# Two embedding products moved one pass earlier, six blocks multiplied earlier, two rows scaled on ScalarE

## The chip, the core and the metric

The kernel runs on one core of a Trainium2 chip. The metric is the device time of one execution in microseconds (us). Besides the execution times there is one profiled execution of the kernel before.

## What is computed

One layer with sliding-window attention, then a gated embedding, then a norm. The change touches only what follows the attention's output product, where `x` has 512 rows and 2048 columns:

```python
x = x + y                                        # y: the attention's output product
emb = p[i] @ ple_proj[i]                         # 512x256 @ 256x2048
g = jax.nn.sigmoid(rmsnorm(x, ple_norm[i]) @ ple_gate[i])   # 512x2048 @ 2048x2048
x = x + emb * g
return rmsnorm(x, final_g)
```

Every float32 product is made of three products of rounded numbers: each operand is split into a high part and the rest (`hi`, `lo`), and hi x hi, hi x lo and lo x hi are summed in PSUM.

## The kernel before

**Blocks.** `x1[j][:, t, :]` holds rows 128t to 128t+127 and columns 512j to 512j+511 of `x`, for t and j from 0 to 3: 16 blocks. "Row t" below means these 128 rows.

**The gate product** uses Strassen's seven products over a two by two division. They are passes, in the order P2, P7, P1, P6, P5, P3, P4. Passes P2 to P3 have two units each (`jj` = 0, 1, the two column halves); `unit()` takes four weight pieces, and with each piece 12 matmuls of 128x512 into two PSUM banks (`tb` = 0, 1). P4 is written out by hand in `block()`: half of a unit each, called for (0, 0), (1, 0), (0, 1), and (1, 1) in two parts of 256 columns.

**Weight pieces.** The class `Pieces` (object `B`) runs a list of 128x1024 pieces in order. A piece is loaded on SP's queue (`braw`, three buffers), or has been summed in a `grown` buffer by adding DMAs on POOL's queue. Then ScalarE casts it to its high part (`bhi`, L575) and VectorE subtracts (`blo`, L576). `get(i)` has pieces up to i+2 split and up to i+3 loaded. `bhi` and `blo` have three buffers each, so a cast waits until TensorE is through with the piece three places before. P4's eight pieces are split ahead of use by `split_last(k)` (L583, L584) into tiles `spare`, `last`, `low`; the dictionary `early` says after which piece of which unit.

**The embedding.** `embed(t, w, tag)` makes one block of `emb`: six matmuls into a bank of the pair `tag`. Passes P1, P5, P3 have two such blocks behind each unit, from one piece of `ple_proj`: P1 gates rows 0 and 1 in columns j = 0, 1; P5 rows 2 and 3 in j = 2, 3; P3 rows 0 and 1 in j = 2, 3; P4 rows 2 and 3 in j = 0, 1. P5 and P3 use the same two pieces of `ple_proj`, and load and split them twice. PSUM has four pairs of banks, s, p, t and o. P1, P6, P5 and P3 add up their gate products in s and p; the embeddings take t for the first unit and o for the second.

**Gating a block** is a generator in three steps, `gated()`: sigmoid on ScalarE (L896); multiply by `emb` and add to `x` on VectorE (L898, L899); square with a sum on ScalarE (L902). `gate()` first adds the products that belong to the block.

**Order.** From P7 on the order of all five engines is the order of the program text. What belongs to a finished unit is put on the list `later`, and `some_later()` runs a share of it after each of the four pieces of the next unit. So the instruction queues of ScalarE and VectorE mix the casts and subtractions of coming pieces with the gating of the unit before. `Forms.steps` adds the left operands of the next pass (`hT`, `fhg`, `flg`; L668, L680, L681).

**The last norm.** `rsqrt_mean()` makes 1/sqrt of the mean square: the mean on VectorE, `rt` by a square root on ScalarE (L158), then a correction step on VectorE. It is called for rows 0 and 1 together once P3 is gated, and for row 2. Row 3 has its own lines at the end (L1088 to L1094). The square root and the sigmoid need different tables, so ScalarE loads a table before each of them (`ACT_TABLE_LOAD`). A block is finished by `row()`, one VectorE instruction that multiplies by the root and by the weights `fg` (L920), or by `by_gain()` (L912, by the weights, on VectorE) and a later multiplication by the root. `store()` sends it out on SP's queue.

Of the kernel before, what the change touches and what calls it, by code (L numbers as in the profile page):

```python
# [11 lines left out]
F32 = mybir.dt.float32  # L12
# [8 lines left out]
P = 128  # L21
KC = D // P
NB = S // P
# [30 lines left out]
def trunk_kernel(ctx: ExitStack, tc: tile.TileContext, a: dict):  # L54
    nc = tc.nc

    def pool(name, bufs=1, **kw):
        return ctx.enter_context(tc.tile_pool(name=name, bufs=bufs, **kw))
# [3 lines left out]
    const = pool("const")  # L62
# [18 lines left out]
    def bank(name, tag):  # L81
        return others.get(tag, psum).tile([P, 512], F32, tag=tag, name=name)
# [34 lines left out]
    def mm3(ps, sh, sl, mh, ml, first, last, more=False):  # L117


        nc.tensor.matmul(ps, sh, mh, start=first, stop=False, skip_group_check=more)  # L120
        nc.tensor.matmul(ps, sh, ml, start=False, stop=False, skip_group_check=more)  # L121
        nc.tensor.matmul(ps, sl, mh, start=False, stop=last, skip_group_check=more)  # L122
# [23 lines left out]
    def run(gen):  # L146
        for _ in gen:
            pass

    def rsqrt_mean(out, ssq, n, nm):  # L150

        w = out.shape[-1]
        ms = const.tile([P, w], F32, name=f"ms_{nm}")
        rt = const.tile([P, w], F32, name=f"rt_{nm}")
        y = const.tile([P, w], F32, name=f"y_{nm}")
        t = const.tile([P, w], F32, name=f"t_{nm}")
        nc.vector.tensor_scalar(ms, ssq, 1.0 / n, EPS, op0=ALU.mult, op1=ALU.add)
        nc.scalar.activation(rt, ms, AF.Sqrt)  # L158
        yield
        nc.vector.reciprocal(y, rt)  # L160
        nc.vector.tensor_mul(t, y, y)
        nc.vector.tensor_mul(t, t, ms)
        nc.vector.tensor_scalar(t, t, -0.5, 1.5, op0=ALU.mult, op1=ALU.add)
        nc.vector.tensor_mul(out, y, t)
# [20 lines left out]
    for k in range(KC):  # L185
# [9 lines left out]
        room = acts if k < KC // 2 else more  # L195
# [14 lines left out]
        f, e = k == 0, k == KC - 1  # L210
# [8 lines left out]
        for t in range(2):  # L219
            c = slice(t * P, (t + 1) * P)  # L220
            mm3(kt_ps[t], wh[:, c], wl[:, c], h, l, f, e)
        for t in range(NB):
            c = slice(t * P, (t + 1) * P)
# [8 lines left out]
        if 3 <= k < 3 + NB:  # L232
            t = k - 3
# [283 lines left out]
    def blk(t):  # L517
        return slice(t * P, (t + 1) * P)
# [9 lines left out]
    def block(nm, r, c, jj, m):  # L528
        return a[nm][2 * (c - 1) + jj, 4 * (r - 1) + m]

    SUMS = [("w_out", 7), ("w_out", 5), ("w_out", 6), ("ple_gate", 7), ("ple_gate", 5)]
    for nm, p in SUMS:
        for jj in range(2):
            for m in range(4):
                t = summed[nm, p, jj, m] = tc.dram_tile([P, WE], F32, name=f"{nm}_{p}_{jj}_{m}")
# [12 lines left out]
    class Pieces:  # L548
# [38 lines left out]
        done = 0  # L587
# [26 lines left out]
    def add_stage(nm, order):  # L614
        at = {}

        def add_embeds(p, jj):
            if nm == "ple_gate" and p in (1, 5, 3, 4):
                j = jj + 2 * (p in (5, 3))
                B.add("proj", a["ple_proj"].rearrange("(k p) d -> p k d", p=P)[:, :, j * 512 : (j + 1) * 512])  # L620

        for p in order:
            for jj in range(2):
                if nm == "ple_gate" and (p, jj) == (4, 0):
                    for v in range(2):
                        at["e", v] = len(B.specs)
                        add_embeds(p, v)
                at[p, jj] = len(B.specs)
                for m in range(4):
                    if (nm, p) in SUMS:  # L630
                        src = summed[nm, p, jj, m]
                    else:
                        src = block(nm, *{1: (1, 1), 2: (2, 1), 3: (2, 2), 6: (1, 1), 4: (2, 1)}[p], jj, m)
                    growing = (6, 4) if (nm, 6) in SUMS else (7, 6, 4)
                    kind = "seed" if p == growing[0] else "grow" if p in growing else "one"
                    B.add(kind, src, (nm, jj, m) if p in growing else None)
                if p != 4:
                    add_embeds(p, jj)
        return at
# [108 lines left out]
    late = pool("late", reuse_waits="tile")  # L748
    rooms.append(late)
    x1s = late.tile([P, 4, NB, 512], F32, name="x1s")  # L750
    x1 = [x1s[:, j] for j in range(4)]
    fg = late.tile([P, D], F32, name="fg")
    pTh = late.tile([P, 2, S], F32R, name="pTh")
    pTl = late.tile([P, 2, S], F32R, name="pTl")
    ssq2 = const.tile([P, NB, 4], F32, name="ssq2")
    ssq3 = const.tile([P, NB, 5], F32, name="ssq3")

# [12 lines left out]
    later = []  # L770
# [26 lines left out]
    def partial(nm):  # L797
        return late.tile([P, 2, 2, 512], F32, tag="partial", name=nm, bufs=2)
# [45 lines left out]
    for n, p in enumerate(ORDER_OUT):  # L844
        nxt = out_forms.steps(ORDER_OUT[n + 1]) if n < 6 else iter(())
        for jj in range(2):
# [3 lines left out]
            def todo():  # L850
                part = x_at.get((p, jj, next(calls)))
                if part is not None:
                    load_x(part)
                next(nxt, None)
                if p == 4:
                    for tag in "to":
                        if turns:
                            turn(*turns.pop(0), tag)
                    if jj:
                        next(ple_first, None)  # L860
# [21 lines left out]
    nc.vector.tensor_sub(pTl, pT, pTh.bitcast(F32))  # L882
    done = {t: 0 for t in range(NB)}

    def embed(t, w, tag, c=slice(0, 512)):
        e_ps = bank(f"e{t}_{done[t]}", tag)
        for k in range(2):
            mm3(e_ps[:, c], pTh[:, k, blk(t)], pTl[:, k, blk(t)], w[0][k][:, c], w[1][k][:, c], k == 0, k == 1)
        return e_ps
# [18 lines left out]
    def gain(j):  # L908
        return fg[:, j * 512 : (j + 1) * 512]

    def by_gain(t, j):
        nc.vector.tensor_mul(x1[j][:, t, :], x1[j][:, t, :], gain(j))  # L912

    def store(t, j):
        nc.sync.dma_start(a["out"][t * P : (t + 1) * P, j * 512 : (j + 1) * 512], x1[j][:, t, :])

    def row(t, j, yn):

        xt = x1[j][:, t, :]
        nc.vector.scalar_tensor_tensor(out=xt, in0=xt, scalar=yn, in1=gain(j), op0=ALU.mult, op1=ALU.mult)  # L920

    s2, s7 = partial("s2"), partial("s7")
    turns = [(kp, 1) for kp in range(4)]

    def gate(p, jj, ps, e):
# [17 lines left out]
                zs.append((tb, 2 + jj, ps[tb], late.tile([P, 512], F32, tag="junk", name=f"z{jj}_{tb}", bufs=3)))  # L943
        return [gated(*z, e[z[0]]) for z in zs]

    def gate_later(*v):
        zs = gate(*v)
        later[:0] = [partial_of(next, z, None) for _ in range(3) for z in zs]
# [2 lines left out]

    spare = late.tile([P, 2 * WE], F32R, name="spare")
    rooms4 = {}
    early = {(5, 0, 3): 0, (5, 1, 2): 1, (5, 1, 3): 2, (3, 0, 1): 3, (3, 0, 3): 4, (3, 1, 0): 5, (3, 1, 2): 6}

    def split_last(k):
        if k == 0:
# [4 lines left out]
        lo = late.tile([P, WE], F32R, tag="grown", name=f"low{k}", bufs=8)  # L962
        B.split_last(k, rooms4[(k - 1) // 2][:, (k - 1) % 2 * WE : ((k - 1) % 2 + 1) * WE], lo)

    for n, p in enumerate(ORDER_PLE[:-1]):
        if n == 1:

            ctx.enter_context(
                tc.manual_schedule(
                    engines={getattr(mybir.EngineType, v) for v in ("PE", "SP", "DVE", "Activation", "Pool")}  # L970
                )
            )
        nxt = ple_forms.steps(ORDER_PLE[n + 1])
        for jj in range(2):
            calls = iter(range(4))

            def todo():
                k = early.get((p, jj, next(calls)))
                if turns:
                    turn(*turns.pop(0), "s")  # L980
                    if not turns:
                        nc.vector.tensor_reduce(ss2, ssq2, axis=AX.X, op=ALU.add)
                        run(rsqrt_mean(rstd2, ss2, D, "r2"))
                    return
                next(nxt, None)
                if p == 2:
                    next(nxt, None)
                if k is not None:
                    split_last(k)

            ps = unit(p, jj, at_ple, ple_forms, todo)
            e = {}
            if p in (1, 5, 3):
                w = B.get(at_ple[p, jj] + 4)
                for t in (0, 1) if p in (1, 3) else (2, 3):
                    e[t] = embed(t, w, "to"[jj])
            if (p, jj) != (3, 1):
                later.insert(0, partial_of(gate_later, p, jj, ps, e))
        run(nxt)
    while later:  # L1000
        later.pop(0)()
# [2 lines left out]
    w = [B.get(at_ple["e", jj]) for jj in range(2)]  # L1004
    f = ple_forms.made[4]
# [26 lines left out]
    yn2 = const.tile([P, 3], F32, name="yn2")  # L1032
# [4 lines left out]
    g = block(0, 0, "s", "o")()  # L1037
    run(root)
    next(g)
    for j in range(4):  # L1040
        row(0, j, yn2[:, 0:1])
        store(0, j)
    next(g)
    run(g)
    for j in range(4):
        row(1, j, yn2[:, 1:2])
        store(1, j)
    g = block(1, 0, "s", "t")()
    next(g)
    for j in (2, 3):  # L1050
        by_gain(2, j)
    next(g)
    run(g)
    for j in (2, 3):
        by_gain(3, j)
    nc.vector.tensor_reduce(ssum[:, 2:], ssq3[:, 2, :4], axis=AX.X, op=ALU.add)
    root = rsqrt_mean(yn2[:, 2:], ssum[:, 2:], D, "r4")
    next(root)
# [9 lines left out]
    next(g)  # L1068
    run(g)

    base, ms, rt, im, ys, nw, yn = (const.tile([P, 1], F32, name=f"{v}_3") for v in ("base", "ms", "rt", "im", "ys", "nw", "yn"))
    g = block(1, 1, "p", "t", slice(0, 256))()
    next(g)
    by_gain(3, 0)
# [86 lines left out]
```

## Time and profile before

| | us |
|---|---|
| median of 3 runs (lowest to highest) | 804.19 (804.07 to 805.76) |
| the profiled execution's own time | 804.26 |
| its span, first to last instruction | 802.4 |
| busy: TensorE, VectorE, ScalarE, GpSimd | 791.1, 592.1, 500.5, 110.1 |

PE is TensorE, DVE VectorE, ACT ScalarE, SPq the queue of SP. A timeline row has the start, the duration (both us), engine, line, operation, the tiles written and read, the shape, and the number of equal instructions; a bracket gives the idle time before it and what ended it. Matmuls are pipelined: a row of 0.39 us starts 0.23 us after the one before. Times are counted from the span's start.

### The profile page before, as it was taken

How to read it: one execution, taken by the hardware profiler on the slowest of the kernel's cores; microseconds unless marked ns; L12 is line 12 of the kernel's file. 1: busy time of each engine (PE TensorE's matmuls, PEld its weight loads, DVE VectorE, ACT ScalarE, POOL GpSimd, SP SyncE). 2: the span in 40 equal slices, each digit the busy share in tenths (PEclk: the TensorE clock that was granted, in tenths of full speed). 3: DMA queues.
4: the chain of work that ended last, by engine and by line, in shares of the span. 5: the costliest groups of instructions: out<-in, count | busy, mean ns of one | idle time of the engine just before them, and what ended most of it. 6: DMA issues, size and time to landing. Idle time of an engine off the chain costs nothing. (4 is left out here: it accounts for less than half of the span.)

```text
span 802.4 us, 10946 instructions
## 1 busy us (share of the span) xinstructions
PE 791.1 (99%) x3763; PEld 660.0 (82%) x3763; DVE 592.1 (74%) x970; ACT 500.5 (62%) x1041; POOL 110.1 (14%) x218
## 2 busy tenths in 40 slices
PE   9999999999999999999999999999999999999995
PEld 7888888888888888888888888888888888888785
DVE  4536886887777776777778897766646756989896
ACT  5624667676667666676666654655668656656855
POOL 0002213122122212112122200030000020200000
PEclk9999999999999999999999999999999999999998
DMA  8863678778687977868685369898513996785532
GB/s 318 327 172 101 183 241 215 228 202 233 172 220 215 218 215 199 221 177 246 159 219 132 105 233 348 333 275 248 195 46 92 372 216 197 156 229 182 182 107 105
DMA packets 45239, 165.15 MB, mean 206 GB/s; under 512 B 5936, under 2 KB 8112, under 8 KB 41344
## 3 DMA queue, kind: packets, MB, share of 16 engines
q1 hardware_dynamic: 38352, 130.59, 47.9%
q0 software_dynamic: 6832, 33.88, 22.4%
q8 instruction: 29, 0.48, 0.2%
q14 instruction: 26, 0.21, 0.1%
HBM read 158.63 MB, written 46.19 MB: 255 GB/s over the span
## 5 line engine op out<-in xcount | busy, mean ns | idle before, releaser
L576 DVE TENSOR_TENSOR blo<-braw,bhi 128x1024 fp32r<-128x1024 f32 x80 | 97.5, 1222 | 39.7 <-ACT bhi L575 39.4
L575 ACT CAST bhi<-braw 128x1024 fp32r<-128x1024 f32 x80 | 84.0, 1051 | 65.8 <-PE g L122 18.9
L122 PE MATMUL gps<-xh,wlo 128*128 128x512 f32 x256 | 100.1, 391 | 0.0
L121 PE MATMUL gps<-xl,whi 128*128 128x512 f32 x256 | 100.1, 391 | 0.0
L120 PE MATMUL gps<-xh,whi 128*128 128x512 f32 x256 | 99.8, 390 | 0.0
L107 DVE TENSOR_TENSOR wlo<-wraw,whi 128x1024 fp32r<-128x1024 f32 x60 | 73.3, 1221 | 20.8 <-ACT whi L106 19.7
L122 PE MATMUL qps<-xh,wlo 128*128 128x512 f32 x224 | 87.8, 392 | 0.0
L120 PE MATMUL o<-bhi,fho 128*128 128x512 f32 x224 | 87.7, 391 | 0.0
L121 PE MATMUL qps<-xl,whi 128*128 128x512 f32 x224 | 87.7, 391 | 0.0
L121 PE MATMUL o<-blo,fho 128*128 128x512 f32 x224 | 87.3, 390 | 0.0
L122 PE MATMUL o<-bhi,flo 128*128 128x512 f32 x224 | 87.2, 389 | 0.0
L120 PE MATMUL qps<-xh,whi 128*128 128x512 f32 x224 | 87.2, 389 | 0.0
L106 ACT CAST whi<-wraw 128x1024 fp32r<-128x1024 f32 x60 | 62.9, 1048 | 26.9 <-PE gps L121 10.6
L418 ACT ACTIVATE t<-t,sm 128x129 f32<-128x129 f32 x128 | 50.6, 397 | 45.9 <-DVE sm L415 45.6
L121 PE MATMUL g<-blo,fhg 128*128 128x512 f32 x192 | 75.0, 391 | 0.7 <-DVE blo L576 0.7
L120 PE MATMUL g<-bhi,fhg 128*128 128x512 f32 x192 | 75.1, 391 | 0.0
L122 PE MATMUL g<-bhi,flg 128*128 128x512 f32 x192 | 74.8, 390 | 0.0
L443 POOL TENSOR_SCALAR_AFFINE_SELECT own<-r 64x512 fp32r<-64x512 f32 (+1 forms) x48 | 34.1, 711 | 291.7 <-DVE r L434 286.2
L122 PEld LDWEIGHTS gps<-xh,wlo 128*128 128x128 f32 x256 | 48.0, 188 | 10.3
L576 DVE TENSOR_TENSOR blo<-grown,bhi 128x1024 fp32r<-128x1024 f32 x32 | 39.1, 1223 | 23.6 <-ACT bhi L575 21.9
L120 PEld LDWEIGHTS gps<-xh,whi 128*128 128x128 f32 x256 | 48.1, 188 | 8.9
L121 PEld LDWEIGHTS gps<-xl,whi 128*128 128x128 f32 x256 | 48.1, 188 | 8.9
(200 smaller groups left out, 1698.0 us busy)
## 6 DMA issues: line engine op xcount, KB each, us to landing
wraw<-in_w_gate_in SPq DMA_DIRECT2D x32, 512.0 KB, 5.6
wraw<-in_w_q SPq DMA_DIRECT2D x28, 512.0 KB, 4.5
w_out<-in_w_out POOLq DMA_DIRECT2D x24, 512.0 KB, 7.4
braw<-in_w_out SPq DMA_DIRECT2D x24, 512.0 KB, 4.3
braw<-in_ple_gate SPq DMA_DIRECT2D x24, 512.0 KB, 4.3
w_out<-in_w_out SPq DMA_DIRECT2D x16, 512.0 KB, 6.7
ple_gate<-in_ple_gate SPq DMA_DIRECT2D x16, 512.0 KB, 5.5
ple_gate<-in_ple_gate POOLq DMA_DIRECT2D x16, 512.0 KB, 7.2
```

The lines of the kernel that those rows point to most:

```text
L106: nc.scalar.copy(hi, raw)
L107: nc.vector.tensor_sub(lo, raw, hi.bitcast(F32))
L120: nc.tensor.matmul(ps, sh, mh, start=first, stop=False, skip_group_check=more)
L121: nc.tensor.matmul(ps, sh, ml, start=False, stop=False, skip_group_check=more)
L122: nc.tensor.matmul(ps, sl, mh, start=False, stop=last, skip_group_check=more)
L418: nc.scalar.activation(su, su, AF.Exp, bias=sm[:, u : u + 1], accum_out=sm[:, 2 + u : 3 + u])
L443: nc.gpsimd.affine_select(out=flat(own), in_=flat(r).bitcast(F32), pattern=[[0, 8], [sign, HB]], compare_op=ALU.is_ge, fill=0.0, base=-HB ...
L575: nc.scalar.copy(hi, raw)
L576: nc.vector.tensor_sub(lo, raw, hi.bitcast(F32))
```

## The change

1. The embedding of rows 0 and 1 for P3 is made in P5, from the piece that is there for rows 2 and 3. P3's two pieces of `ple_proj`, with their loads and splits, go. The products (named `k`) take the other pair of banks, and `keep()` copies them on ScalarE to SBUF: the first unit's to a new tile `kept0`, the second's into the part of `s7` that is free by then. P3's gating reads them there.
2. Six blocks are multiplied by the last norm's weights in P5, through `later`: rows 0 and 1, j = 0, 1, and (2, 2), (3, 2). The blocks j = 0, 1 of rows 0 and 1 are then scaled by the root on ScalarE, in `rows()`, before the blocks j = 2, 3 on VectorE.
3. The small tiles `ms`, `rt`, `y`, `t` of `rsqrt_mean` share one buffer each over all calls, and with row 3's `ms`, `rt`, `im`, `nw`.
4. `early` moves four of P4's splits in P3.

```diff
     def rsqrt_mean(out, ssq, n, nm):
         w = out.shape[-1]
-        ms = const.tile([P, w], F32, name=f"ms_{nm}")
-        rt = const.tile([P, w], F32, name=f"rt_{nm}")
-        y = const.tile([P, w], F32, name=f"y_{nm}")
-        t = const.tile([P, w], F32, name=f"t_{nm}")
+        ms = const.tile([P, NB], F32, tag="ms", name=f"ms_{nm}")[:, :w]
+        rt = const.tile([P, NB], F32, tag="rt", name=f"rt_{nm}")[:, :w]
+        y = const.tile([P, NB], F32, tag="y", name=f"y_{nm}")[:, :w]
+        t = const.tile([P, NB], F32, tag="t", name=f"t_{nm}")[:, :w]
...
-            if nm == "ple_gate" and p in (1, 5, 3, 4):
-                j = jj + 2 * (p in (5, 3))
+            if nm == "ple_gate" and p in (1, 5, 4):
+                j = jj + 2 * (p == 5)
...
+    kept0 = late.tile([P, 2, 512], F32, name="kept0")
...
+    def rows(t):
+        for j in range(4):
+            if j < 2:
+                nc.scalar.mul(x1[j][:, t, :], x1[j][:, t, :], yn2[:, t : t + 1])
+            else:
+                row(t, j, yn2[:, t : t + 1])
+            store(t, j)
...
+    kept = {}
+
+    def keep(jj, e):
+        room = s7[:, 0] if jj else kept0
+        kept[jj] = [room[:, t] for t in range(2)]
+        for t in range(2):
+            nc.scalar.copy(kept[jj][t], e[t])
...
-    early = {(5, 0, 3): 0, (5, 1, 2): 1, (5, 1, 3): 2, (3, 0, 1): 3, (3, 0, 3): 4, (3, 1, 0): 5, (3, 1, 2): 6}
+    early = {(5, 0, 3): 0, (5, 1, 2): 1, (5, 1, 3): 2, (3, 0, 3): 3, (3, 1, 0): 4, (3, 1, 1): 5, (3, 1, 3): 6}
...
+    by_gain_at = {(6, 1): [(t, j) for j in range(2) for t in range(2)], (5, 0): [(2, 2), (3, 2)]}
...
-            if p in (1, 5, 3):
+            if p in (1, 5):
                 w = B.get(at_ple[p, jj] + 4)
-                for t in (0, 1) if p in (1, 3) else (2, 3):
+                for t in (0, 1) if p == 1 else (2, 3):
                     e[t] = embed(t, w, "to"[jj])
+            if p == 3:
+                e = kept[jj]
+            if p == 5:
+                later.insert(0, partial_of(keep, jj, [embed(t, w, "to"[1 - jj], nm="k") for t in range(2)]))
             if (p, jj) != (3, 1):
                 later.insert(0, partial_of(gate_later, p, jj, ps, e))
+            for t, j in by_gain_at.get((p, jj), ()):
+                later.append(partial_of(by_gain, t, j))
...
-    for j in range(4):
-        row(0, j, yn2[:, 0:1])
-        store(0, j)
+    rows(0)
     next(g)
     run(g)
-    for j in range(4):
-        row(1, j, yn2[:, 1:2])
-        store(1, j)
+    rows(1)
     g = block(1, 0, "s", "t")()
     next(g)
-    for j in (2, 3):
-        by_gain(2, j)
+    by_gain(2, 3)
     next(g)
     run(g)
-    for j in (2, 3):
-        by_gain(3, j)
+    by_gain(3, 3)
...
-    base, ms, rt, im, ys, nw, yn = (const.tile([P, 1], F32, name=f"{v}_3") for v in ("base", "ms", "rt", "im", "ys", "nw", "yn"))
+    base, ys, yn = (const.tile([P, 1], F32, name=f"{v}_3") for v in ("base", "ys", "yn"))
+    ms, rt, im, nw = (const.tile([P, NB], F32, tag=v, name=f"{v}_3")[:, :1] for v in ("ms", "rt", "y", "t"))
```

More of the change, by code (lines that the diff above doesn't have):

```diff
@@ L883, in trunk_kernel, with embed @@
     done = {t: 0 for t in range(NB)}
-    def embed(t, w, tag, c=slice(0, 512)):
-        e_ps = bank(f"e{t}_{done[t]}", tag)
+    def embed(t, w, tag, c=slice(0, 512), nm="e"):
+        e_ps = bank(f"{nm}{t}_{done[t]}", tag)
         for k in range(2):
```

## The prediction

> **What bounds the kernel now.** I read the page first (busy times), then the list of waits, then TensorE's timeline over the last 95 us, then the timelines of VectorE and ScalarE beside it.
>
> ```profile
> span 802.4 us, 10946 instructions
> PE 791.1 (99%) x3763; PEld 660.0 (82%) x3763; DVE 592.1 (74%) x970; ACT 500.5 (62%) x1041; POOL 110.1 (14%) x218
> PE g L121 <- DVE blo L576: 0.7, 1, 0.7
> ```
>
> TensorE is busy for 99% of the span, and the one wait of any size behind the start is 0.7 us for a weight piece's low half. So work taken off VectorE or ScalarE is worth nothing by itself. There are only two places where this change can move the end: TensorE's own waits, and what follows its last matmul. Both have rows.
>
> ```profile
> 710.07 0.39 PE L120 MATMUL g<-bhi,fhg 128*128 128x512 f32 x1
> 723.67 0.39 PE L120 MATMUL g<-bhi,fhg 128*128 128x512 f32 x1
> 750.87 0.39 PE L120 MATMUL g<-bhi,fhg 128*128 128x512 f32 x1
> 751.93 0.50 PE L121 MATMUL g<-blo,fhg 128*128 128x512 f32 x1 [0.68 <-DVE blo L576]
> 752.27 0.40 PE L122 MATMUL g<-bhi,flg 128*128 128x512 f32 x1
> 755.15 0.40 PE L122 MATMUL g<-bhi,flg 128*128 128x512 f32 x1
> 765.64 0.39 PE L120 MATMUL last<-spare,fhg 128*128 128x512 f32 x1
> 792.39 0.28 PE L122 MATMUL last<-last,flg 128*128 128x256 f32 x1
> ```
>
> Four of these rows are starts: 710.07 of P5's first unit, 723.67 of its second, 750.87 of P3's second, 765.64 of P4. A unit with its embedding has 48 + 12 = 60 matmuls. The first takes 13.60 us, so one matmul takes 0.2267, a weight piece (12 matmuls) 2.72, a unit without embedding 10.88. Four such units from 710.07 would end at 764.47, but P4 starts at 765.64: P3's second unit is **1.17 us late** (14.77 against 13.60), at the gap before 751.93 and in the slow rows behind it.
>
> ```profile
> 792.71 0.42 DVE L1018 TENSOR_TENSOR s<-last,s 128x256 f32<-128x256 f32 x1
> 793.17 0.51 ACT L896 ACTIVATE s<-s,rstd 128x256 f32<-128x256 f32 x1 [2.83 <-DVE s L1018]
> 793.70 1.28 ACT L1088 ACT_TABLE_LOAD   x1
> 794.98 0.08 DVE L904 DVE_READ_ACCUMULATOR s<-x1s 128x1 f32 x1
> 795.10 0.29 ACT L1088 ACTIVATE rt<-ssq,base 128x1 f32<-128x1 f32 x1
> 795.57 0.22 DVE L1092 SCALAR_TENSOR_TENSOR nw<-rt,im 128x1 f32<-128x1 f32 x1
> 796.09 0.87 DVE L1097 TENSOR_SCALAR x1s<-x1s,ys,nw 128x512 f32<-128x512 f32 x2
> 797.90 0.43 SPq L915 DMA_DIRECT2D out<-x1s  x1
> ```
>
> This is the end: last matmul of the gate (ends 792.67), gate, last sum of squares (ready 795.06), root at 795.10, scaling, last store at 797.90. The table load that the root needs runs from 793.70 to 794.98, beside VectorE's multiply, add and square, and costs nothing today.
>
> **Term 1: the wait in P3 goes.** Its cause:
>
> ```profile
> 750.66 1.22 DVE L576 TENSOR_TENSOR blo<-braw,bhi 128x1024 fp32r<-128x1024 f32 x1
> ```
>
> This piece is ready at 751.88, while TensorE wanted it at 751.10 (750.87 + 0.23); VectorE was behind. The change takes two embedding pieces out of P3 (a cast of about 1.05 and a subtraction of 1.22 each, and a 512 KB load each on SP's queue) and gives P5's units 2.72 us more of TensorE's time. I followed VectorE's and ScalarE's new orders through P3 with the durations quoted here and below. The same piece is then ready about 2.5 us ahead of TensorE, and the tightest one, third of that unit, about 1 us ahead. So **-1.17** (at least -0.83, the bare gap 751.10 to 751.93). The two loads themselves are worth nothing: no row shows TensorE waiting for a DMA here.
>
> **Term 2: a new wait in P5's second unit.** P5's first unit now ends with 24 embedding matmuls: `e` in bank pair t, the new `k` in bank pair o. The second unit's `e` goes into pair o, so its first matmul must wait until ScalarE has copied the first `k` to `kept0`. In the changed kernel's instruction order, with the semaphores, this matmul does wait for that copy. On ScalarE the copy is queued behind both sums of squares of the gate (the second waits for VectorE's second addition), one cast of a last piece, and one cast of P3's first piece. The rows that time this chain are those of the same unit before:
>
> ```profile
> 723.87 1.05 ACT L575 CAST bhi<-braw 128x1024 fp32r<-128x1024 f32 x1 [1.67 <-PE e L122]
> 734.35 0.63 ACT L902 ACTIVATE s<-x1s 128x512 f32<-128x512 f32 x1 [0.60 <-DVE x1s L899]
> 734.98 1.04 ACT L583 CAST last<-grown 128x1024 fp32r<-128x1024 f32 x1
> 735.92 1.05 ACT L575 CAST bhi<-braw 128x1024 fp32r<-128x1024 f32 x1
> 662.26 1.07 ACT L933 COPY s<-g 128x512 f32<-128x512 f32 x2
> 724.95 1.23 DVE L576 TENSOR_TENSOR blo<-braw,bhi 128x1024 fp32r<-128x1024 f32 x1 [0.77 <-ACT bhi L575]
> 726.10 1.28 DVE L940 TENSOR_TENSOR s<-g,s 128x512 f32<-128x512 f32 x2
> 727.29 0.68 DVE L681 TENSOR_TENSOR flg<-hT,fhg 128x512 fp32r<-128x512 f32 x1
> 727.89 1.22 DVE L576 TENSOR_TENSOR blo<-braw,bhi 128x1024 fp32r<-128x1024 f32 x1
> 731.58 0.68 DVE L898 TENSOR_TENSOR s<-e,s 128x512 f32<-128x512 f32 x1
> 732.30 0.69 DVE L899 TENSOR_TENSOR x1s<-x1s,s 128x512 f32<-128x512 f32 x1
> 732.91 0.68 DVE L898 TENSOR_TENSOR s<-e,s 128x512 f32<-128x512 f32 x1
> ```
>
> From start to start: subtraction 1.15, the two gate additions 1.19, small form 0.60, multiply 0.72, add 0.61, square 0.63, cast 0.94. The chain begins when TensorE is through with the embedding, which frees a weight buffer: a cast starts 0.20 behind that (723.67 to 723.87), its subtraction 1.08 later. TensorE's second unit starts at 710.07 + 72 x 0.2267 = 726.39. VectorE then has, without a gap: subtraction from 727.67, gate additions from 728.82, form 730.01, subtraction 730.61, multiply 731.75, add 732.47, form 733.08, subtraction 733.68, multiply 734.82, add 735.54, done at 736.23. ScalarE: square 736.26, cast 736.89, cast 737.83, copy 738.78, which lasts 0.59. TensorE can go on at about 739.43, and gets there at 726.39 + 10.88 = 737.27: a wait of **2.16**. The slow rows behind the old wait (0.34 from 751.93 to 752.27, against 0.23) come again: +0.15. Eleven spacings that repeat within 0.05 leave 1.8 to 2.6. Behind TensorE's stop everything in the stage moves with it. The second copy ends 0.53 after the first, in time for its bank. The copies of the second unit go through pair t, which P4 needs much later.
>
> **Term 3: the root's table load loses its cover.** To make room, the small tiles `ms`, `rt`, `y`, `t` now share buffers. So the last root writes a tile that ScalarE wrote before, and has two waits instead of one: for VectorE's last sum of squares, and for ScalarE itself. The built order shows what becomes of them: the wait for VectorE stands as an instruction of its own, ahead of the table load, where before it sat on the root behind the load. So the load starts when the sum is ready, 795.10 on today's clock, instead of at 793.70, and the root starts 1.28 + 0.02 later. Root to `nw` to first scaled block is a chain, so the last store moves as much: **+1.30** (1.2 to 1.4). The root for row 2 gets the same, but there VectorE waits for TensorE:
>
> ```profile
> 773.26 2.74 DVE L920 SCALAR_TENSOR_TENSOR x1s<-x1s,yn,fg 128x512 f32<-128x512 f32 x4
> 780.50 1.28 DVE L912 TENSOR_TENSOR x1s<-x1s,fg 128x512 f32<-128x512 f32 x2
> 784.88 0.69 DVE L1018 TENSOR_TENSOR s<-last,s 128x512 f32<-128x512 f32 x1 [0.32 <-PE last L122]
> 787.32 1.32 ACT L1066 ACTIVATE x1s<-x1s,yn 128x512 f32<-128x512 f32 x2
> 777.36 0.64 ACT L902 ACTIVATE s<-x1s 128x512 f32<-128x512 f32 x1 [3.08 <-DVE x1s L899]
> 770.74 1.28 ACT L158 ACT_TABLE_LOAD   x1
> 772.03 0.20 ACT L158 ACTIVATE rt_r<-ms_r 128x2 f32<-128x2 f32 x1
> ```
>
> **What costs nothing.** The 24 matmuls of P3's embedding move to P5; TensorE's work stays the same. P4's last splits come later, the last about 3 us before TensorE takes it, by the same count. Rows 0 and 1 lose four scalings on VectorE (0.68 each) and two multiplications (0.64) from the stretch before 784.88. VectorE already waits 0.32 for TensorE there, so nothing of it reaches the end; it pays for row 2's later root. Four scalings of 0.66 on ScalarE (as at 787.32) fall into idle time like the 3.08 before 777.36. In P5 VectorE gets 4 + 2 multiplications: even all four before one piece (2.56) stay under that piece's slack (subtraction done 726.18, TensorE takes it at 723.67 + 5.44 = 729.11: 2.93). Without that cover each would cost TensorE 0.64. Stores of rows 0 and 1 leave SP later, over 10 us ahead of the end.
>
> **Sum**, against the profiled execution's 804.26 us (0.07 above the median 804.19): -1.17 + 2.16 + 0.15 + 1.30 = +2.44, so **806.7 us**, 0.3% slower. Its own bounds, 1.8 to 2.6 and 1.2 to 1.4 and -1.17 to -0.83, give 806.1 to 807.4.
>
> [...] Row: the load at 770.74 lasts 1.28, starts right behind ScalarE's last instruction, and the root follows at 772.03, so 1.29 in all. [...]
>
> **Rivals.**
> - *The bank is free in time.* Not slower: if ScalarE's first copy ends by 737.27, term 2 vanishes and -1.17 + 1.30 gives 804.4. It decides at one instruction, the second square, which would have to start 2.2 us earlier. For it: ScalarE has idle time around it. Against: the order on both queues is fixed. Chance 0.12.
> - *The load stays covered*, if the wait's place on the chip is not what the built order says: 2.31 - 1.17 gives 805.4. For it: no row before shows such a pair. Chance 0.11.
> - *A switch costs more when nothing runs beside it*: as much again as the load, 1.28, gives 808.0. Against it: 770.74 to 772.03 above, where ScalarE did nothing else. Chance 0.04.
> - *VectorE falls behind in P5* instead of P3, and a weight piece is late there as one was at 751.88; a second wait like the old one adds 1.17: 807.9. Chance 0.07.
> - *Neither new wait comes*: only term 1, 803.1, within 0.2%. Chance 0.04.
>
> **The numbers.** The forecast as summed has 0.62. 0.2% (1.6 us, so 802.6 and 805.8) is about what a measurement of this kernel can tell from no change. Slower by more: forecast 0.62, alone-standing switch 0.04, VectorE 0.07, and 0.02 of the covered load, which lies 0.4 below the bound: 0.75. Within: 0.11 of the free bank, 0.09 of the covered load, 0.02 of the last: 0.22. Faster by more: 0.01 of the free bank and 0.02 of the last, if the gain in P3 is larger than its rows show: 0.03. The range reaches down to the covered load less 0.2 for its bounds, and up to the two cases above: 805.2 to 808.0.
>
> **What would show it.** Right: in the list of waits TensorE's `e` of P5's second unit waits for ScalarE's `kept` copy by about 2.2 us; no wait of `g` in P3; P4's first matmul at about 766.8; at the end the table load starts after VectorE's last accumulator read. Wrong: no wait at that `e`, or a table load still beside VectorE's multiply; then the time is at or under 805.4.

## The result and the profile after

The changed kernel takes 807.23 us (median of 8 runs, 806.28 to 810.51); the kernel before, beside it on the same chip, 804.73 (8 runs, 803.75 to 805.76). The ratio is 1.0039, with a 95% interval of 1.0021 to 1.0056: slower, by 3.1 us (1.7 to 4.5). The forecast was 806.7, 2.4 us slower, with a range of 805.2 to 808.0. The profiled execution of the changed kernel took 809.95 us, with a span of 808.0; for one execution that is within the range of the others, near its upper end.

The page of the changed kernel, and a line of its list of waits (us in total, times, longest):

```profile
span 808.0 us, 10944 instructions
PE 793.0 (98%) x3763; PEld 661.4 (82%) x3763; DVE 589.8 (73%) x968; ACT 502.9 (62%) x1047; POOL 111.5 (14%) x218
PE e L120 <- ACT kept L961: 2.0, 1, 2.0
```

The wait of `g` in P3 is gone from that list, and the forecast wait of `e` for the `kept` copy is there. On ScalarE the copy stands where the prediction had it, behind the second square and two casts:

```profile
737.86 0.63 ACT L903 ACTIVATE s<-x1s 128x512 f32<-128x512 f32 x1 [2.34 <-DVE x1s L900]
738.49 1.03 ACT L583 CAST last<-grown 128x1024 fp32r<-128x1024 f32 x1
739.42 1.04 ACT L575 CAST bhi<-braw 128x1024 fp32r<-128x1024 f32 x1
740.37 1.06 ACT L961 COPY kept<-k 128x512 f32<-128x512 f32 x2
```

TensorE's timeline of the changed kernel shows what the wait cost:

```profile
727.99 0.39 PE L120 MATMUL g<-bhi,fhg 128*128 128x512 f32 x1
...
741.00 0.61 PE L120 MATMUL e<-bhi,pTh 128*128 128x512 f32 x1 [1.97 <-ACT kept L961]
741.40 0.63 PE L121 MATMUL e<-blo,pTh 128*128 128x512 f32 x1
741.83 0.63 PE L122 MATMUL e<-bhi,pTl 128*128 128x512 f32 x1
...
769.95 0.39 PE L120 MATMUL last<-spare,fhg 128*128 128x512 f32 x1
...
796.70 0.28 PE L122 MATMUL last<-last,flg 128*128 128x256 f32 x1
```

P5's second unit starts at 727.99 where the prediction had 726.39: this execution was 1.60 behind already, in waits between 60 and 84 us that no edit touches. So times are best read as distances. From P5's second unit to P4's first matmul there are 168 matmuls, 38.08 us at 0.2267 each; here they take 41.96, so TensorE lost **3.88** there. The stop at 741.00 is 2.36 from the start before it, 2.13 more than a spacing. And then, which nobody had forecast, the matmuls behind it start 0.43 apart instead of 0.23. Here is the changed kernel us by us (PEclk, the figure behind POOL's, is the clock that TensorE was granted, as a share of full speed):

```profile
core 0: us, PE busy (x) PEld busy (x) DVE busy (x) ACT busy (x) POOL busy (x), PEclk, DMA share, GB/s
740.00:741.00 1.00, 0.01 (x1) 0.01 (x1) 1.00 (x2) 1.00 (x3) 0.00 (x0) 1.00 0.00 0
741.00:742.00 1.00, 1.00 (x3) 0.79 (x4) 1.00 (x2) 1.00 (x2) 0.00 (x0) 0.62 0.00 0
742.00:743.00 1.00, 1.00 (x4) 0.81 (x3) 1.00 (x2) 1.00 (x2) 0.00 (x0) 0.50 0.15 37
743.00:744.00 1.00, 1.00 (x4) 0.71 (x4) 1.00 (x2) 0.32 (x1) 0.00 (x0) 0.50 0.90 307
744.00:745.00 1.00, 1.00 (x5) 0.83 (x4) 1.00 (x2) 0.00 (x0) 0.00 (x0) 0.68 0.49 188
```

The clock was granted at half speed. The last four rows miss 0.38 + 0.50 + 0.50 + 0.32 = 1.70 of full speed, so the half clock lasted twice that, 3.40 us.

The end, on ScalarE and VectorE of the changed kernel:

```profile
799.29 0.08 DVE L905 DVE_READ_ACCUMULATOR s<-x1s 128x1 f32 x1
799.45 1.28 ACT L1109 ACT_TABLE_LOAD   x1 [1.46 <-DVE s L905]
800.75 0.29 ACT L1109 ACTIVATE rt<-ssq,base 128x1 f32<-128x1 f32 x1
```

The table load now waits for VectorE's accumulator and has nothing beside it. From the end of the last matmul of the gate (796.98) to the end of the span it is 11.02 us; before it was 802.4 - 792.67 = 9.73.

### The profile page after: what moved, and what is told of

It reads as the page before. It is cut to its first block, busy times and chain, and to the rows that moved or that the text cites. A ratio compares the mean times of both kernels' runs of the same rounds, so it can differ in the third digit from the quotient of the medians.

```text
span 808.0 us, 10944 instructions
## 1 busy us (share of the span) xinstructions
PE 793.0 (98%) x3763; PEld 661.4 (82%) x3763; DVE 589.8 (73%) x968; ACT 502.9 (62%) x1047; POOL 111.5 (14%) x218
## 5 line engine op out<-in xcount | busy, mean ns | idle before, releaser
L575 ACT CAST bhi<-braw 128x1024 fp32r<-128x1024 f32 x78 | 82.0, 1052 | 70.3 <-PE g L122 18.4
L576 DVE TENSOR_TENSOR blo<-braw,bhi 128x1024 fp32r<-128x1024 f32 x78 | 95.3, 1222 | 41.6 <-ACT bhi L575 41.3
```

Source lines behind the costliest of these rows:

```text
L575: nc.scalar.copy(hi, raw)
L576: nc.vector.tensor_sub(lo, raw, hi.bitcast(F32))
```

## The experiments

Two distances are read from the profile of each kernel: **lost**, what the stretch from P5's second unit to P4's first matmul takes beyond 0.2267 per matmul (168 matmuls; 180, or 40.80 us, where P3 still makes its embedding), and the **tail**, from the end of the last gate matmul to the end of the span. The kernel before has 1.17 and 9.73; "sum" is what both together are above that. The span is read to 0.1 us, so a tail can be off by 0.05. "Measured" is the ratio's distance from 1 times the kernel before, with its interval.

| kernel | lost | tail | sum | measured, us |
|---|---|---|---|---|
| changed | 3.88 | 11.02 | +4.00 | +3.1 (1.7 to 4.5) |
| the same, run again | 3.88 | 10.99 | +3.97 | +3.4 (2.3 to 4.6) |
| own root tile | 2.28 | 9.90 | +1.28 | +1.9 (1.2 to 2.7) |
| copy first | 0.00 | 10.98 | +0.08 | +0.1 (-0.6 to 0.8) |
| both of these | 0.00 | 9.81 | -1.09 | **-1.1 (-1.9 to -0.4)** |
| before, shared tiles | 0.81 | 11.76 | +1.67 | +1.9 (1.1 to 2.5) |
| short wait | 1.58 | 11.67 | +2.35 | +2.3 (1.4 to 3.4) |
| long wait | 3.20 | 11.03 | +3.33 | +4.5 (3.1 to 5.9) |
| both, without part 2 | 0.00 | 12.81 | +1.91 | +2.2 (1.1 to 3.3) |
| before, with part 2 | 3.65 | 9.70 | +2.45 | +1.9 (0.8 to 3.0) |
| seven us of wait | 9.76 | 10.95 | +9.81 | +8.3 (7.0 to 9.5) |

**Own root tile.** The changed kernel with `rt` of row 3 in a tile of its own, so that the last root has one wait.

```diff
-    base, ys, yn = (const.tile([P, 1], F32, name=f"{v}_3") for v in ("base", "ys", "yn"))
-    ms, rt, im, nw = (const.tile([P, NB], F32, tag=v, name=f"{v}_3")[:, :1] for v in ("ms", "rt", "y", "t"))
+    base, ys, yn, rt = (const.tile([P, 1], F32, name=f"{v}_3") for v in ("base", "ys", "yn", "rt"))
+    ms, im, nw = (const.tile([P, NB], F32, tag=v, name=f"{v}_3")[:, :1] for v in ("ms", "y", "t"))
```

> The changed kernel, with a tile of its own for the last root; every other shared small tile stays. Theory (the second wait pushes the first one in front of the table load): the load runs beside VectorE's multiply again and the time is 1.3 us under the changed kernel's (807.2 to about 805.9); from last gate matmul to the end of the span 9.7 us instead of 11.0. Rival (the end is longer because sharing adds waits all along it): the load moves, but the end stays within 0.3 us of 11.0. TensorE's wait for the copy stays at about 2 us in both.

806.8 us (11 runs, 805.13 to 807.79), ratio 1.0024 (1.0015 to 1.0033). From its timeline:

```profile
739.92 0.50 PE L120 MATMUL e<-bhi,pTh 128*128 128x512 f32 x1 [1.97 <-ACT kept L961]
740.26 0.39 PE L121 MATMUL e<-blo,pTh 128*128 128x512 f32 x1
740.49 0.40 PE L122 MATMUL e<-bhi,pTl 128*128 128x512 f32 x1
...
795.33 1.28 ACT L1109 ACT_TABLE_LOAD   x1
796.61 0.08 DVE L905 DVE_READ_ACCUMULATOR s<-x1s 128x1 f32 x1
796.73 0.29 ACT L1109 ACTIVATE rt<-ssq,base 128x1 f32<-128x1 f32 x1
```

The load is back beside VectorE, and the tail is 9.90. The same wait as in the changed kernel costs 2.28 here: 2.13, and most of the rest (0.11) in one slow row. No half clock followed it. So term 3 comes from the shared `rt` tile, by the second wait it brings to the last root, and the half clock does not follow from the length of this wait alone.

**Copy first.** The changed kernel with the copies to `kept` ahead of the gating of the unit, instead of behind it. `later` gets one entry, which runs the copies and then the same `gate_later`.

```diff
+    def copy_then_gate(first, *v):
+        if first:
+            first()
+        gate_later(*v)
...
-                later.insert(0, partial_of(keep, jj, [embed(t, w, "to"[1 - jj], nm="k") for t in range(2)]))
+                first = partial_of(keep, jj, [embed(t, w, "to"[1 - jj], nm="k") for t in range(2)])
...
-                later.insert(0, partial_of(gate_later, p, jj, ps, e))
+                later.insert(0, partial_of(copy_then_gate, first, p, jj, ps, e))
```

> The changed kernel, with the two copies of the kept products put in front of the gate's steps instead of behind them. Theory (the copy is late because of its place on ScalarE's queue, and the slow matmuls behind it come from the wait): no wait of e in P5's second unit, no stretch of 0.43 us per matmul, P5 and P3 at 0.2267 us per matmul; 2.1 + 1.8 us less than the profiled execution of the changed kernel, 803.3 to 804.7 by the median. Rival (the slow stretch comes from what else runs at that time, the copies and casts on ScalarE and the transfers): the wait goes, but slow matmuls stay there, and only about 2 us are gained.

804.85 us (11 runs), ratio 1.0001 (0.9993 to 1.001). TensorE waits for nothing between P5 and the end, and the stretch takes 38.08 us, to the last digit what 168 spacings make. The tail is still 10.98.

**Both.** The two edits above together.

> Both: the copies first, and a tile of its own for the last root. If the three terms add up, only the removed wait in P3 is left: 1.2 us under the kernel before, about 803.5. If early copies bring back a late weight piece in P5 or P3 (VectorE or ScalarE behind by 1 us), it is level with the kernel before, 804.5 to 805.

803.46 us (11 runs, 802.93 to 805.26), ratio 0.9986 (0.9977 to 0.9995): faster than the kernel before, by about the 1.17 that P3's wait had cost. The end of it:

```profile
792.12 1.28 ACT L1114 ACT_TABLE_LOAD   x1
793.40 0.08 DVE L905 DVE_READ_ACCUMULATOR s<-x1s 128x1 f32 x1
793.52 0.29 ACT L1114 ACTIVATE rt<-ssq,base 128x1 f32<-128x1 f32 x1
```

With these four the terms can be told apart by the measured ratios alone. The wait: changed less copy first, 0.38%, and own tile less both, 0.38%, that is 3.1 us each, 0.8 above the 2.28 of a wait without half clock, and 0.8 below the 3.88 with it. The tile: copy first less both, 0.15%, 1.2 us, and changed less own tile, 0.15%. So the two add up, as far as intervals of about 0.1% on each ratio can tell.

**Before, shared tiles.** The kernel before with nothing but part 3 of the change.

> The kernel before, with only the small tiles of the roots shared. Theory: the last table load starts behind the last sum of squares and the time is 1.3 us over the kernel before, 806.0; nothing else moves. Rival (the shared tiles cost nothing by themselves, the end grew because rows 0 and 1 are scaled on ScalarE): within 0.3 us of the kernel before.

806.25 us (11 runs), ratio 1.0023 (1.0014 to 1.0031): 1.9 us slower, where the uncovered load alone makes 1.3. Its timeline:

```profile
785.97 0.16 DVE L160 RECIPROCAL y_r<-rt_r 128x1 f32<-128x1 f32 x1 [0.93 <-ACT rt_r L158]
...
793.05 0.42 DVE L1018 TENSOR_TENSOR s<-last,s 128x256 f32<-128x256 f32 x1
...
795.47 1.28 ACT L1089 ACT_TABLE_LOAD   x1 [1.46 <-DVE s L904]
```

The last load is uncovered as in the changed kernel. But row 2's root, later by the same load, now makes VectorE wait 0.93, and VectorE never gets that back: it takes up the last product at 793.05, 0.91 behind the end of the last matmul (792.14), where before it was 0.04 behind (792.71 to 792.67). So row 2's later root is not free by itself; part 2 of the change has to make room for it. (P3's wait, which this edit doesn't touch, cost 0.81 in this profile and 1.17 in that of the kernel before.) In the changed kernel VectorE waits 1.01 for TensorE at that place:

```profile
789.18 0.69 DVE L1044 TENSOR_TENSOR s<-last,s 128x512 f32<-128x512 f32 x1 [1.01 <-PE last L122]
```

**Short wait.** The changed kernel with one of P4's casts moved from P5's second unit into P3, so that it doesn't stand ahead of the copy.

```diff
-    early = {(5, 0, 3): 0, (5, 1, 2): 1, (5, 1, 3): 2, (3, 0, 3): 3, (3, 1, 0): 4, (3, 1, 1): 5, (3, 1, 3): 6}
+    early = {(5, 0, 3): 0, (5, 1, 3): 1, (3, 0, 1): 2, (3, 0, 3): 3, (3, 1, 0): 4, (3, 1, 1): 5, (3, 1, 3): 6}
```

> The changed kernel, with the cast of one of P4's pieces taken from between the second square and the kept copies (it comes one weight piece later). Theory: e of P5's second unit waits 0.94 us less, 1.2 instead of 2.1. If the granted clock falls only behind a long wait, no stretch of 0.43 us per matmul follows, and the time is that of the kernel before + 1.2 + 0.1 - 1.2 + 1.3 = 1.4 us over it. Rival (the clock falls behind any wait, or by chance): up to 1.8 us more in part of the runs.

807.06 us (12 runs), ratio 1.0029 (1.0017 to 1.0042). The wait fell by 0.94, as one cast makes (2.0 to 1.0 in the list of waits), without a half clock in the profiled execution. But the sum, +2.35, is no lower than the changed kernel's would be without half clock (+2.40). VectorE, which has the cast's subtraction later too, shows why:

```profile
787.14 0.16 DVE L160 RECIPROCAL y_r<-rt_r 128x1 f32<-128x1 f32 x1 [0.80 <-ACT rt_r L158]
...
794.23 0.42 DVE L1044 TENSOR_TENSOR s<-last,s 128x256 f32<-128x256 f32 x1
```

TensorE was through at 793.43; VectorE takes up the product 0.80 later, behind a wait for row 2's root. Time saved on TensorE brings P4 forward against VectorE's list, which did not get shorter.

**Long wait.** The copies of the first unit placed by hand, one of P4's casts later.

```diff
+                if (p, jj, k) == (5, 1, 2):
+                    held.pop(0)()
...
-                later.insert(0, partial_of(keep, jj, [embed(t, w, "to"[1 - jj], nm="k") for t in range(2)]))
+                held[jj] = partial_of(keep, jj, [embed(t, w, "to"[1 - jj], nm="k") for t in range(2)])
+                if jj:
+                    later.insert(0, held.pop(1))
```

> The changed kernel, with the first unit's kept copies put behind one more cast on ScalarE. Theory: e of P5's second unit waits 0.94 us more, 3.1; if the granted clock falls the surer the longer the wait, the stretch of half clock is there, and the time is 3.1 + 1.9 - 1.2 + 1.3 = 5.1 us over the kernel before. Rival (the stretch has nothing to do with the wait): 3.2 us over it.

810.33 us (6 runs), ratio 1.0056 (1.0039 to 1.0073). The profiled execution, at 807.74 one of the two fastest (807.65 and 807.74; the other four are at 809.88 to 810.91), has a longer wait and no half clock behind it. Their mean granted clock is 0.997 in these two, 0.991 to 0.995 in the other four. That would fit half clock behind this wait in the four, but no profile shows it, and 0.995 is also the mean of the profiled execution of "copy first", which has no wait there. The profiled one:

```profile
740.41 0.50 PE L120 MATMUL e<-bhi,pTh 128*128 128x512 f32 x1 [2.91 <-ACT kept L961]
740.75 0.40 PE L121 MATMUL e<-blo,pTh 128*128 128x512 f32 x1
740.98 0.39 PE L122 MATMUL e<-bhi,pTl 128*128 128x512 f32 x1
```

**The changed kernel again**, three more times, unchanged.

> The changed kernel unchanged, for a second profile and more times beside the two above. If the stretch at half clock comes in a part of the executions only, the times fall in two groups about 1.8 us apart, 2.3 and 4.1 us over the kernel before; if it comes always, one group at 4.1.

> The changed kernel unchanged, one more look. The wait of e is 2.1 us as before; the stretch at half clock, seen in both looks at this kernel and not in two other kernels with as long a wait, comes in a part of the looks.

> The changed kernel unchanged, another look. The wait of e is 2.1 us; the stretch at half clock comes in a part of the looks, and with it some 1.8 us.

The first: 808.42 us (6 runs, 806.78 to 809.95, not in two clear groups), ratio 1.0042 (1.0028 to 1.0057); the other two are one profiled execution each, 809.14 and 808.08. All three profiles have the wait of 1.97 and a half clock behind it; the last one's windows:

```profile
739.00:740.00 1.00, 1.00 (x4) 0.82 (x5) 1.00 (x2) 1.00 (x2) 0.00 (x0) 0.79 0.00 0
740.00:741.00 1.00, 1.00 (x4) 0.71 (x4) 1.00 (x3) 1.00 (x2) 0.00 (x0) 0.50 0.44 70
741.00:742.00 1.00, 1.00 (x4) 0.81 (x3) 1.00 (x1) 0.17 (x1) 0.00 (x0) 0.50 0.80 274
742.00:743.00 1.00, 1.00 (x4) 0.81 (x3) 1.00 (x2) 0.00 (x0) 0.00 (x0) 0.51 0.49 197
```

Twice what is missing is 3.40 us again (3.42 in the two others). It begins some 0.2 us behind the wait in the first profile of the changed kernel, and 0.7 to 1.5 behind it in these three. The loss in the stretch was 3.88, 3.88, 3.90 and 3.86, against 2.28 without half clock: the half clock costs **1.6 us**.

**Seven us of wait.** The changed kernel with the first unit's copies made six times over.

> The changed kernel, with the first unit's two kept copies made six times over, so that e of P5's second unit waits about 7 us. Theory (a wait of about 2 to 3 us brings the half clock only if it falls well against a fixed window, a wait longer than two such windows always): the stretch at 0.43 us per matmul is there. Rival (it comes by chance in half of the runs, whatever the wait): it may be missing. The time is 7.0 + 1.9 - 1.2 + 1.3 = 9 us over the kernel before, or 7.1 without the stretch.

814.04 us (4 runs), ratio 1.0103 (1.0087 to 1.0118). The wait is 6.85, the gap 7.00 beyond a spacing, and the half clock is there from the first matmul on:

```profile
744.56 0.80 PE L120 MATMUL e<-bhi,pTh 128*128 128x512 f32 x1 [6.85 <-ACT kept L961]
745.16 0.63 PE L121 MATMUL e<-blo,pTh 128*128 128x512 f32 x1
745.58 0.63 PE L122 MATMUL e<-bhi,pTl 128*128 128x512 f32 x1
```

By the granted clock it begins at 739.94 already, 2.2 us into the stop, and lasts until 750.18. From TensorE's return on it costs 9.76 - 7.00 = 2.76. The median lies between the sums with and without it (+9.81 and +7.1).

**Both, without part 2.** The fastest kernel with `by_gain_at` empty and all blocks of rows 0 and 1 scaled by `row()`, as before.

> The two mends (copies first, own tile for the last root), and the second part of the change undone: no block multiplied by the weights in P5, rows 0 and 1 scaled on VectorE as before. The prediction held that this part is worth nothing at the end: then it is level with both mends, 1.1 us under the kernel before. Rival (with P4's splits and P3's gating moved to its start, VectorE is late in P4, and needs this part to be on time when row 2's root and the last block come): 1 to 2.5 us slower than both mends, with VectorE no longer waiting for TensorE ahead of row 2's root.

807.54 us (10 runs), ratio 1.0027 (1.0014 to 1.0041): 0.41%, or 3.3 us, above the same kernel with part 2. TensorE loses nothing, but in P4 VectorE is behind. In this kernel:

```profile
786.70 0.68 DVE L1046 TENSOR_TENSOR s<-last,s 128x512 f32<-128x512 f32 x1
...
788.39 0.16 DVE L160 RECIPROCAL y_r<-rt_r 128x1 f32<-128x1 f32 x1 [1.01 <-ACT rt_r L158]
...
795.48 0.42 DVE L1046 TENSOR_TENSOR s<-last,s 128x256 f32<-128x256 f32 x1
```

and in "both", with part 2:

```profile
783.30 0.69 DVE L1049 TENSOR_TENSOR s<-last,s 128x512 f32<-128x512 f32 x1 [1.22 <-PE last L122]
...
791.13 0.42 DVE L1049 TENSOR_TENSOR s<-last,s 128x256 f32<-128x256 f32 x1
```

With part 2 VectorE waits 1.22 for TensorE, and takes up the last product 0.04 behind its last matmul (791.09). Without it the wait is gone, and the last product is taken up 2.99 behind (792.49).

**Before, with part 2.** The kernel before with nothing but part 2 of the change.

> The kernel before, with only the second part of the change: six blocks multiplied by the weights in P5, rows 0 and 1 scaled half on ScalarE. Theory (VectorE already waits for TensorE ahead of row 2's root there, so relief is worth nothing): within 0.4 us of the kernel before, and that wait of VectorE grows from 0.3 to over 2 us. Rival A (relief is worth something by itself): 1 us or more faster. Rival B (the six multiplications make weight pieces in P5 or P3 later): TensorE's wait for a low half in P3 grows and it is up to 1 us slower.

807.61 us (11 runs), ratio 1.0023 (1.001 to 1.0037): slower. A line of its list of waits, and its timeline at the seam of P5 and P3:

```profile
PE g L121 <- DVE blo L576: 2.6, 3, 1.2
```

```profile
739.64 1.29 DVE L912 TENSOR_TENSOR x1s<-x1s,fg 128x512 f32<-128x512 f32 x2
...
755.69 0.50 PE L121 MATMUL g<-blo,fhg 128*128 128x512 f32 x1 [1.24 <-DVE blo L576]
```

Two of the six multiplications stand between the subtractions for P3's first pieces. VectorE was already late there in the kernel before; now three pieces come late, and TensorE loses 3.65 where it lost 1.17. That is rival B, and more than the 1 us it was given. In P4 the theory held: VectorE's wait for TensorE ahead of row 2's root grew from 0.32 to 2.76 (at 788.61), and the tail is the old one, 9.70. So the relief of P4 is worth nothing to the kernel before. Parts 1 and 2 carry each other: without part 1, and part 4 with it, the multiplications have no room in P5 and P3, and without part 2 P4 has too much work on VectorE.

## Why the prediction was right, step by step

**Term 1** (-1.17) held. The wait of `g` in P3 is absent from the lists of all kernels that make P3's embedding in P5, and "both" is faster by 1.1 us (0.4 to 1.9).

**Term 2** (a wait of 2.16) held at 2.13, with the order and the spacings on both queues as followed. TensorE went on at 741.00, which is 739.40 without the 1.60 that this execution was late at the start; the forecast was 739.43. The list named the right instruction, and copying first took the whole wait away.

**The step that failed in size** was the one behind it, "the slow rows behind the old wait (...) come again: +0.15". Without half clock they cost that (2.28 - 2.13). But in all four profiled executions of the changed kernel the granted clock fell to one half for 3.4 us, and in the first the step cost 1.75; P4 started at 768.35 on the prediction's clock (769.95 - 1.60), not at 766.8. The kernel before, on whose rows the step rested, has a gap of only 0.83. Two sums therefore bracket the result: -1.17 + 2.28 + 1.29 = +2.40 without half clock, +4.00 with it, and the measured +3.1 and +3.4 lie between. By the mean granted clock some executions probably went without it: 3.4 us at half speed take 0.002 from the mean granted clock, which is 0.993 to 0.995 in the four profiled ones, 0.996 to 0.998 in the kernel before, and 0.997 in two others of the changed kernel (806.28 and 807.95). With half clock in every execution the sum of +4.00 would give 804.26 + 4.00 = 808.3, above the range, so it is in part luck that the measured time lies inside. (The prediction's own bounds, 806.1 to 807.4, leave out its 0.15; with it they are 806.2 to 807.6.)

**Term 3** (+1.30) held at 1.29 in the tail, and with an own tile all but 0.17 of it went. The load cost no more with nothing beside it, so the rival of a costlier switch (808.0) did not occur: ScalarE is released at 799.45, the load takes 1.28, and the root runs at 800.75, 1.30 in all. ScalarE stood idle for 1.46 before this load; in the prediction's row at 770.74 it did not, and there it is 1.29.

**What costs nothing** was right for the changed kernel and wrong in its reason. "Nothing of it reaches the end" was said of the four scalings and two multiplications that part 2 takes out of P4. Left out of "both", part 2 costs 3.3 us. The step left out that P3 gets shorter. TensorE gives up 24 matmuls in P3, 5.44 us; VectorE gives up two subtractions, 2.44. So VectorE's list slides by up to 3.0 us towards P4: rows 0 and 1 are ready for their root 5.38 behind P4's start before (771.02 - 765.64), and 7.76 behind it in "both" (771.82 - 764.06). The first row is the kernel before, the second "both":

```profile
771.02 0.15 DVE L1034 TENSOR_REDUCE ssum<-ssq 128x2 f32<-128x8 f32 x1
...
771.82 0.15 DVE L1065 TENSOR_REDUCE ssum<-ssq 128x2 f32<-128x8 f32 x1
```

The slack of 0.32 that the prediction quoted would not have held that. Part 4 pushes the same way, with one more of P4's splits in P3's second unit; no run separates it from part 1. What part 2 gave made up for the slide and for row 2's root. The prediction had neither the slide nor the worth of part 2, and it was luck that the two cancelled. "It pays for row 2's later root" was right: without part 2 that root cost 0.7 us in "before, shared tiles" (11.76 against 11.02).

**The rivals.** Three of them are kernels now: the bank free in time (forecast 804.4, "copy first" has 804.85), the load that stays covered (forecast 805.4, "own root tile" has 806.8, +1.9 where its sum is +1.28; half clock in a part of its executions would explain that, but its one profile has none), and neither new wait (forecast 803.1, "both" has 803.46). VectorE's falling behind did not occur in the changed kernel; it did where part 2 stood alone, in P3 rather than in P5.

## What to carry to other kernels

A bank's reader must be queued where the bank is next wanted, not where its value is: one copy behind two squares and two casts cost TensorE 2.1 us, and the same copy ahead of them nothing. A small tile that was shared to save room brought its next writer a second wait, and the second wait pulled a table load out from under its cover, for 1.3 us: look at where the wait stands in the built order, not only at whether it is there. When work leaves one engine's stage, compare what each of the other engines loses there: the one that is relieved of less arrives late in the next stage, here by 2.38 us (7.76 against 5.38 behind P4's start).

## What the runs showed of the hardware

A stop of TensorE of 1.97 us (2.13 beyond a spacing) was followed by half clock in four profiled executions out of four of one kernel (3.40 to 3.42 us long, beginning 0.2 to 1.5 us behind the stop), by none in a kernel with the same stop at about the same place, and by none behind a stop of 2.91 (3.07). In a stop of 6.85 (7.00) it began after 2.2 us and lasted 10.24 us.

The traces show what separates them. In every profile the clock falls to half once more behind the last matmul (in the changed kernel it is 0.50 in every row from 803 to the end). One row each of the changed kernel, of "own root tile" and of "long wait":

```profile
802.00:803.00 1.00, 0.00 (x0) 0.00 (x0) 1.00 (x4) 1.00 (x2) 0.00 (x0) 0.84 0.00 0
...
797.00:798.00 1.00, 0.00 (x0) 0.00 (x0) 0.74 (x4) 0.61 (x3) 0.00 (x0) 0.90 0.00 0
...
800.00:801.00 1.00, 0.00 (x0) 0.00 (x0) 0.97 (x3) 0.82 (x2) 0.00 (x0) 0.67 0.20 78
```

Twice what is missing from full clock, counted back from the row's end, gives the beginning: 802.68 in the changed kernel, 797.80 and 800.34 in the others. In the same way the half clock in P5 of the changed kernel begins at 741.24. From there to 802.68 it is 61.44 us, 18 times 3.413. In the three other profiles of this kernel the distance is 58.02 or 58.03, 17 times 3.413, and with the seven us of wait 64.85, 19 times. These distances differ by 3.41 to 3.42, which is also the length of the half clock (3.40 to 3.42). So the beginnings of these five profiles lie as if they stood at the ends of windows of 3.413 us that run on through the kernel, and counted back from the beginning at the end such windows can be laid over each stop:

| profile | idle within one window, us | half clock next |
|---|---|---|
| changed, and again three times | 1.97, 1.97, 1.93, 1.97 | yes |
| seven us of wait | 2.22, then a whole window | yes |
| own root tile | 1.82, then 0.15 | no |
| long wait | 1.40, then 1.51 | no |
| short wait | 1.02 | no |

Half clock followed 1.93 us of idle time or more in one window, and never 1.82 or less; the long wait was cut in two by a window's end. So a stop of 1.97 was enough where it fell into one window, and one of 2.91 was not where a window's end cut it. The windows behind the last matmul agree in all 14 profiles: half clock followed one with 2.02 us of idle time (the kernel before) or more, and never one with 1.57 (the changed kernel) or less. The ends of matmuls are modelled, so these idle times are the profile's. Whether a window counts idle time or work done isn't shown.

An estimate from this: if the windows fall at random against a stop of 1.97, 1.93 of it lie in one window in (3.41 - 1.97 + 2 x 0.04) / 3.41 = 0.45 of the executions, and 0.51 if 1.82 is enough. Half clock in about half of the executions is what the measured times say too: the 0.8 of 1.6 that the wait cost beyond 2.28. By this estimate four profiles out of four were chance.
